# First loads and last stores of an encoder block: four DMA edits at the two ends of the kernel

## The chip, the cores and the metric

The kernel runs on one core of a Trainium2 chip. The metric is the device time of one execution in microseconds (us); where several executions are given, their median. A profile is one execution recorded by the hardware profiler; its span runs from the first to the last instruction, and its own execution time is a little longer than its span.

## The reference, cut to what matters

One encoder layer on x of 1024 tokens by 1024 channels, all float32:

```python
h = rms_norm(x, norm1_g)
a, gate, q, k, v = split(h @ w_in)             # 512 columns each
conv_out = conformer_conv(a, gate, ...)        # GLU, 31-tap depthwise conv, LayerNorm, swish
attn_out = neighbourhood_attention(rms(q), rms(k), v, rpb)
x = x + concat(conv_out, attn_out) @ w_out
h = rms_norm(x, norm2_g)
x = x + (silu(h @ w_gate) * (h @ w_up)) @ w_down    # 2816 hidden channels
```

What matters here is the first product and the last. The first product is the key projection: the transposed input (scaled by `norm1_g`) times the key columns of `w_in`. The last is `@ w_down`, whose results have the residual added and are stored to the output.

## The kernel before, in words

**Precision.** Every matmul operand is split into a high part (a rounded copy that ScalarE makes, `act.copy` or `act.activation`, L114 and L287) and a low part (the difference, made by VectorE or GpSimd, L118 and L288). A product is three matmuls: high times high (L122), high times the other's low (L123), low times high (L124), in `mac`.

**Order of the work.** The order on each engine is the order in which the code issues it (`manual_schedule`); each engine and each DMA queue works strictly in that order. "SP's queue" is the DMA queue of SyncE (`nc.sync.dma_start`), which does nothing else; "the scalar queue" is that of ScalarE (`nc.scalar.dma_start`), so a DMA there takes ScalarE's issue time. A DMA is ordered by its issue; its bytes are moved by the core's 16 DMA engines. In the profile's rows `SPq` and `ACTq` are these issues.

**The start.** `want` lists weight chunks in the order of use; `issue` loads the next chunk into one of three raw buffers (`R`, 128 x 1024, 512 KB); `take_parts` cuts the chunk's split into parts, and the last part frees the raw buffer and issues one more load. The chunks are the four key chunks `wk0` to `wk3` first, then the convolution chunks `ag10`, `ag00` and so on. `load_xt(0, kp, FIRST)` loads block kp of the transposed input: two 128-row slices of 256 tokens each (256 KB), in the tiles `xt`. `par` is a 73 KB tile of small parameters, loaded on the scalar queue; ScalarE's scaling of `xt` reads it. In the first loop over kp (0 to 3) `h_split` makes the high and low part of an `xt` slice (`hT`), the parts of the `wk` chunk are made between them, and TensorE then does the products of that kp for the first two token tiles into the accumulators `z`. The third buffer's reuse means that `wk3` can be issued only when the last part of `wk0` has been read.

After the four kp, `h_split` makes the second 256 tokens (`SECOND`), row statistics of x are taken by ScalarE and VectorE in turn (`stats1`, `head_post`), `take(1, False)` splits chunk `ag10` (high on ScalarE, low on GpSimd), and TensorE goes on with two more key tiles and then the gate product `gl`, which reads `ag10`.

**The end.** The last product of the down projection, `m4`, has four token tiles t = 0 to 3. `finish` adds each accumulator to `ou` on VectorE (L1351), and `store` writes the 128 x 512 result (256 KB) to the output. The output rows of a tile are not adjacent: `rows` takes them from a grid, so the destination of one store is a pattern of 8 by 16 rows of 512 numbers (2 KB). The four stores of `m4` are all on the scalar queue; those of the other products are on SP's.

The window loads of the attention stage, which the prediction compares with, read a source pattern of 4 by `ncol` rows of 2 KB (`ncol` 32 or 24):

```python
nc.sync.dma_start(vw[cb, g], vd.rearrange("(r c) d -> r c d", c=GW)[g * 4:g * 4 + 4, c0:c0 + ncol, :])
```

Of the kernel before, what the change touches and what calls it, by code (L numbers as in the profile page):

```python
# [13 lines left out]
P = 128  # L14
# [54 lines left out]
def body(tc, a):  # L69
    from contextlib import ExitStack  # L70
    with ExitStack() as ctx:
        build(ctx, tc, a)


def build(ctx, tc, a):
    nc = tc.nc
# [6 lines left out]
    def T(tag, shape, bufs, name, dt=F32):  # L83
        return sb.tile(shape, dt, tag=tag, bufs=bufs, name=name)

    def G(name, dt=F32):
        return T("G", [P, 1024], 22, name, dt)

    def R(name):
        return T("R", [P, 1024], 3, name)  # L90
# [4 lines left out]
    def ST(name, dt=F32):  # L95
        return T("st", [P, 512], 5, name, dt)
# [23 lines left out]
    def mac(acc, l, r, start, stop):  # L120
        (lh, ll), (rh, rl) = l, r
        pe.matmul(acc, lh, rh, start=start, stop=False, skip_group_check=True)  # L122
        pe.matmul(acc, lh, rl, start=False, stop=False, skip_group_check=True)  # L123
        pe.matmul(acc, ll, rh, start=False, stop=stop, skip_group_check=True)  # L124
# [14 lines left out]
    pos = [0, 0]  # L139
# [10 lines left out]
    def issue():  # L150
        if pos[0] < len(chunks):
            src, name, _, _, more = chunks[pos[0]]
            raws[pos[0]] = R(name + "r")
            d = raws[pos[0]]
            if len(src.shape) == 3:
                d = d.rearrange("p (k m) -> p k m", k=src.shape[1])
            nc.sync.dma_start(d, src)
            if more is not None:
                pending.append((d, more))
            pos[0] += 1  # L160

    def take(n=1, ahead=True):
        for _ in range(n):
            i = pos[1]
            while pos[0] <= i:
                issue()
            _, _, dst, sub, _ = chunks[i]
            hi, lo = dst()
            split(hi, lo, raws.pop(i), sub)
            pos[1] += 1  # L170
            if ahead and pos[0] < i + 4:
                issue()

    def take_parts(jobs, n=4, sub=pool):
        i = pos[1]
        hi, lo = chunks[i][2]()
        w = 1024 // n

        def part(o):
            sl = slice(o, o + w)  # L180
            split(hi[:, sl], lo[:, sl], raws[i][:, sl], (sub,))
            if o + w == 1024:
                raws.pop(i)
                issue()
        pos[1] += 1
        jobs.extend(lambda o=o: part(o) for o in range(0, 1024, w))
# [49 lines left out]
    x_t, xr = {}, {}  # L236
    FIRST, SECOND, ALL = slice(0, 256), slice(256, 512), slice(0, 512)

    def load_x(t):
        x_t[t] = G(f"x{t}")  # L240
        nc.sync.dma_start(x_t[t], a["x"][t * P:(t + 1) * P, :])

    def load_xt(h, kp, sl):
        if (h, kp) not in xr:
            xr[h, kp] = G(f"xt{h}{kp}").rearrange("p (k s) -> p k s", s=512)
        nc.sync.dma_start(xr[h, kp][:, :, sl], a["xt"][h, kp][:, :, sl])

    for kp in range(4):
        load_xt(0, kp, FIRST)
        if kp < 3:  # L250
            issue()
    ones = ST("ones")[:, :P]
    ident = T("ident", [P, P], 1, "ident")
    par = T("par", [P, 146], 1, "par")
    nc.scalar.dma_start(par, a["par"])
    g1 = par[:, 0:8]
    dwk = par[:, 8:132].rearrange("p (c t) -> p c t", t=CW)
    dwb, lng, lnb = par[:, 132:136], par[:, 136:140], par[:, 140:144]
# [25 lines left out]
    def h_split(h, k, sl):  # L284
        src = xr[h, k // 2][:, k % 2, sl]
        hi, lo = [w[:, k, sl] for w in hT[h]]
        act.activation(hi, src, AF.Copy, scale=g1[:, k:k + 1])  # L287
        dve.scalar_tensor_tensor(lo, src, g1[:, k:k + 1], hi.bitcast(F32), OP.mult, OP.subtract)  # L288
# [253 lines left out]
    for kp in range(4):  # L542
        parts = []
        take_parts(parts, 2, dve)
        for j in range(2):
            h_split(0, 2 * kp + j, FIRST)
            parts[j]()
        if kp == 0:
            for q in range(4):
                load_xt(0, q, SECOND)  # L550
            load_x(0)
            load_x(1)
        if kp == 2:
            load_x(2)
            load_x(3)
        for j in range(2):
            for t in range(2):
                k = 2 * kp + j
                mac(zs[t], [q[:, k, t * P:(t + 1) * P] for q in hT[0]],
                    [q[:, j * 512:(j + 1) * 512] for q in wn[1][kp]], k == 0, k == KB - 1)  # L560
# [9 lines left out]
    for q in range(4):  # L570
        load_xt(1, q, ALL)
# [280 lines left out]
    def rows(ap, t):  # L852
        rh, cb = divmod(t, 4)
        return ap.rearrange("(h i w) d -> h i w d", h=2, w=GW)[rh, :, cb * 16:cb * 16 + 16, :]
# [309 lines left out]
    gt, bank, sl, u2, late = {}, {}, {}, {}, []  # L1164
# [160 lines left out]

    def store(p, t, w):
        tok, d = {"m2": (0, 0), "m3": (0, 1), "m4": (1, 0), "m7": (1, 1)}[p]
        (nc.scalar if p == "m4" else nc.sync).dma_start(
            rows(a["out"], 4 * tok + t)[:, :, d * 512:(d + 1) * 512], w)

    def quarter(w, o, t):
        return w[:, o + t * 512:o + t * 512 + 512]
# [1 line left out]
    def finish(p, t):  # L1334
        acc = (GA if p in ("m1", "m2", "m7", "m4") else GB)[t]
        if p == "m1":
            if t == 0:
                om["m1"] = H("om1")
            (dve.tensor_copy, act.copy)[t % 2](quarter(om["m1"], 2048, t), acc)
        elif p == "m2":  # L1340
            dve.tensor_tensor(res[p, t], acc, res[p, t], OP.add)
            store(p, t, res[p, t])
        elif p == "m6":
            if t == 0:
                om["u"] = H("ou")
            dve.tensor_tensor(quarter(om["u"], 0, t), acc, quarter(om["m1"], 2048, t), OP.add)
        elif p == "m5":
            dve.tensor_tensor(quarter(om["u"], 2048, t), acc, quarter(om["m1"], 2048, t), OP.add)
        else:
            w = {"m7": quarter(om["u"], 2048, t), "m3": quarter(om["m1"], 2048, t), "m4": quarter(om["u"], 0, t)}[p]  # L1350
            dve.tensor_tensor(w, acc, w, OP.add)  # L1351
            store(p, t, w)
# [48 lines left out]
```

## Time and profile before

| | us |
|---|---|
| Time, median of 3 runs (1049.48 to 1050.58) | 1049.9 |
| The profiled execution's own time | 1050.14 |
| Its span, first to last instruction | 1048.4 |
| TensorE busy (98% of the span) | 1028.2 |
| VectorE busy (69%) | 722.9 |
| ScalarE busy (44%) | 465.3 |
| GpSimd busy (43%) | 452.6 |

The granted TensorE clock is 0.999 over the span. The times of rows in the timeline count from the span's start; a row gives start, duration, engine, line, operation, output and inputs, and in brackets the idle time before it with what ended it. The DMA share is the mean busy share of the 16 DMA engines, so 0.50 means as much work as eight engines kept busy. TensorE's busy time counts pipelined matmuls, whose ends are modelled.

### The profile page before, as it was taken

What the parts mean: (1) busy time and instruction counts of PE and PEld (TensorE: products, weight loads), DVE (VectorE), ACT (ScalarE), POOL (GpSimd) and SP (SyncE); (2) the same over time, 40 slices, a digit from 0 to 9 for tenths busy, and PEclk for the clock granted to TensorE, in tenths of its full rate; (3) what the DMA queues carried; (4) which work ended last, traced back from release to release, by engine and by line L of the source; (5) the groups of instructions that cost most, each with busy time, mean ns of one, the idle gap of its engine ahead of it and who ended that gap; (6) DMA issues with size and microseconds to landing.
All of it is one profiled execution on the core that took longest, in us unless ns stands there. A gap on an engine that the chain in (4) does not pass through costs nothing.

```text
span 1048.4 us, 13903 instructions
## 1 busy us (share of the span) xinstructions
PE 1028.2 (98%) x4972; PEld 833.8 (80%) x4972; DVE 722.9 (69%) x1097; ACT 465.3 (44%) x915; POOL 452.6 (43%) x342
## 2 busy tenths in 40 slices
PE   7999999999999999999999999999999999999997
PEld 5888888776657888778888888888888888888885
DVE  6768998976896575876564655646556567768883
ACT  6466346636776676532232232232322443443441
POOL 0226578833575863655545454455454100002310
PEclk9999999999999999999999999999999999999999
DMA  9496771285536754465232132232232597633641
GB/s 334 178 271 220 225 238 61 77 244 168 148 109 163 159 182 141 109 167 174 104 131 101 71 131 101 89 132 93 99 111 81 207 326 256 205 101 125 215 133 40
DMA packets 74678, 162.93 MB, mean 155 GB/s; under 512 B 13489, under 2 KB 22193, under 8 KB 73905
## 3 DMA queue, kind: packets, MB, share of 16 engines
q1 hardware_dynamic: 67776, 144.14, 40.7%
q0 software_dynamic: 4864, 10.49, 5.9%
q10 hardware_dynamic: 1968, 7.42, 2.0%
q8 instruction: 39, 0.64, 0.2%
q14 instruction: 31, 0.25, 0.1%
HBM read 122.86 MB, written 53.15 MB: 168 GB/s over the span
## 4 chain that ended last, share of the span: by engine, by line
PE 88%; DVE 4%; POOL 2%; DMA 2%; ACT 2%; issue 2%; SPq 0%; POOLq 0%; ACTq 0%; DVEq 0%
PE B L122 5%; PE B L123 5%; PE B L124 5%; PE D L123 4%; PE D L124 4%; PE D L122 4%; PE A L122 3%; PE A L123 3%; PE A L124 3%; PE z L123 3%; PE z L122 3%; PE z L124 3%; PE gl L124 3%; PE gl L123 3%; PE gl L122 3%; PE n L122 3%
## 5 line engine op out<-in xcount | busy, mean ns | idle before, releaser
L347 DVE SCALAR_TENSOR_TENSOR cv<-u,par,cv 128x1009 f32<-128x1009 f32 (+14 forms) x85 | 108.5, 1276 | 2.0
L373 POOL TENSOR_TENSOR pa<-pa,pr 128x1022 f32<-128x1022 f32 (+10 forms) x31 | 75.2, 2426 | 33.7 <-ACT pr L372 32.2
L1356 POOL TENSOR_TENSOR ou<-ou,resm 128x512 f32<-128x512 f32 x8 | 12.5, 1571 | 142.5 <-DMA resm<-xd 142.5
L114 ACT CAST op<-sr 128x512 fp32r<-128x512 f32 x77 | 47.7, 619 | 52.7 <-PE B2d L124 21.3
L118 DVE TENSOR_TENSOR op<-sr,op 128x512 fp32r<-128x512 f32 x77 | 58.2, 756 | 16.4 <-ACT op L114 16.4
L1193 DVE TENSOR_TENSOR g<-B,g 128x512 f32<-128x512 f32 x22 | 15.2, 690 | 71.3 <-PE B L124 68.2
L1202 ACT ACTIVATE D<-D 128x512 f32<-128x512 f32 x22 | 12.8, 582 | 112.5 <-DVE D L1201 112.5
L1185 DVE TENSOR_TENSOR u<-B,g 128x512 f32<-128x512 f32 x22 | 15.2, 691 | 61.0 <-PE B L124 61.0
L668 POOL TENSOR_SCALAR e<-e,rs 128x288 f32<-128x288 f32 (+1 forms) x64 | 35.0, 568 | 45.6 <-DVE rs L666 41.0
L114 ACT CAST op<-wd 128x512 fp32r<-128x512 f32 x66 | 40.9, 620 | 30.4 <-DVE wd L1280 17.4
L118 DVE TENSOR_TENSOR op<-wd,op 128x512 fp32r<-128x512 f32 x66 | 50.5, 765 | 1.9 <-ACT op L114 0.3
L986 DVE TENSOR_TENSOR ts<-ts,gu 128x512 f32<-128x512 f32 x36 | 43.3, 1203 | 0.6
L1191 ACT ACTIVATE A<-A 128x512 f32<-128x512 f32 x18 | 10.5, 582 | 68.6 <-PE A L124 68.6
L661 ACT ACTIVATE e<-e,mx 128x288 f32<-128x288 f32 (+1 forms) x64 | 36.3, 569 | 2.9 <-DVE mx L659 2.8
L659 DVE CUSTOM_DVE_ANT_0 e<-s,tab 128x288 f32<-128x288 f32 (+1 forms) x64 | 29.7, 501 | 8.7 <-PE s L646 8.4
L372 ACT ACTIVATE pr<-u,par 128x1022 f32<-128x1022 f32 (+10 forms) x31 | 34.2, 1135 | 1.2 <-ACT vs L433 1.2
L677 PEld LDWEIGHTS p<-ident,e 128*96 128x96 f32 (+1 forms) x192 | 20.0, 133 | 18.1 <-POOL e L668 10.4
L677 PE MATMUL p<-ident,e 128*96 128x128 f32 (+1 forms) x192 | 28.5, 281 | 2.3 <-DVE pT L682 1.0
L986 DVE TENSOR_TENSOR ts<-gu 128x512 f32<-128x512 f32 x18 | 30.1, 1670 | 0.0
L865 DVE TENSOR_TENSOR x<-x,n 128x512 f32<-128x512 f32 x32 | 21.0, 681 | 13.1 <-PE n L124 13.1
L693 PE MATMUL o<-pT,vw 96*64 96x128 f32 (+1 forms) x384 | 28.0, 281 | 0.0
L646 PE MATMUL s<-kT,qT 64*128 64x288 f32 (+1 forms) x128 | 26.7, 495 | 0.0
(1066 smaller groups left out, 3524.1 us busy)
## 6 DMA issues: line engine op xcount, KB each, us to landing
sr<-sd SPq DMA_DIRECT2D x77, 256.0 KB
gu<-in_gu SPq DMA_DIRECT2D x36, 512.0 KB
sd<-sd SPq DMA_DIRECT2D x22, 512.0 KB
wd<-in_wd SPq DMA_DIRECT2D x44, 256.0 KB
sd<-g SPq DMA_DIRECT2D x33, 256.0 KB
x<-in_x SPq DMA_DIRECT2D x12, 512.0 KB
xd<-x SPq DMA_DIRECT2D x8, 512.0 KB
resm<-xd SPq DMA_DIRECT2D x16, 256.0 KB
```

The source lines that it names most:

```text
L114: act.copy(hi, src)
L118: eng.tensor_tensor(*[w[..., sl] for w in (lo, src, hi.bitcast(F32))], OP.subtract)
L122: pe.matmul(acc, lh, rh, start=start, stop=False, skip_group_check=True)
L123: pe.matmul(acc, lh, rl, start=False, stop=False, skip_group_check=True)
L124: pe.matmul(acc, ll, rh, start=False, stop=stop, skip_group_check=True)
L347: dve.scalar_tensor_tensor(acc[:, o], uc[:, i], dwk[:, c, t:t + 1], acc[:, o], OP.mult, OP.add)
L372: act.activation(pr[:, o], uc[:, i], AF.Copy, scale=dwk[:, c, t:t + 1])
L373: pool.tensor_tensor(pa[:, o], pa[:, o], pr[:, o], OP.add)
L661: act.activation(e[:, hh], e[:, hh], AF.Exp, bias=mx, scale=-1.0, accum_out=rs[:, hh:hh + 1])
L668: pool.tensor_scalar(es[i][:, hh], es[i][:, hh], rs[:, hh:hh + 1], 1.0, op0=OP.mult, op1=OP.mult)
L677: pe.transpose(pt[:m, g * P:(g + 1) * P], es[i][:, hh, g * m:(g + 1) * m], ident)
L986: dve.tensor_tensor(lr(tsum[i, 1])[n - 3] if o is None else o, l, r, OP.add)
```

## The change

Four edits, and the code of the products is not touched.

1. The first weight chunk `wk0` is loaded in two DMAs of 128 x 512, and these now stand ahead of everything else on SP's queue.
2. The first input block `xt` (kp = 0) goes from SP's queue to the scalar queue, behind `par`, which is issued earlier in the code. For kp = 1 and 2 the weight chunk is now issued ahead of the input block instead of behind it.
3. For the first half of kp = 0 the weight part is made before the input slice's split, instead of after it.
4. Of the four `m4` stores t = 0 and 2 stay on the scalar queue, t = 1 goes to SP's, and t = 3 is cut in two stores of 64 partitions, one on each queue; each half's destination has 4 by 16 rows.

```diff
             if len(src.shape) == 3:
                 d = d.rearrange("p (k m) -> p k m", k=src.shape[1])
-            nc.sync.dma_start(d, src)
+            for o in (0, 512) if pos[0] == 0 else (None,):
+                nc.sync.dma_start(*[w if o is None else w[:, o:o + 512] for w in (d, src)])
             if more is not None:
...
-    def load_xt(h, kp, sl):
+    def load_xt(h, kp, sl, eng=nc.sync):
         if (h, kp) not in xr:
             xr[h, kp] = G(f"xt{h}{kp}").rearrange("p (k s) -> p k s", s=512)
-        nc.sync.dma_start(xr[h, kp][:, :, sl], a["xt"][h, kp][:, :, sl])
-
+        eng.dma_start(xr[h, kp][:, :, sl], a["xt"][h, kp][:, :, sl])
+
+    par = T("par", [P, 146], 1, "par")
+    nc.scalar.dma_start(par, a["par"])
     for kp in range(4):
-        load_xt(0, kp, FIRST)
         if kp < 3:
             issue()
+        load_xt(0, kp, FIRST, nc.sync if kp else nc.scalar)
     ones = ST("ones")[:, :P]
     ident = T("ident", [P, P], 1, "ident")
-    par = T("par", [P, 146], 1, "par")
-    nc.scalar.dma_start(par, a["par"])
...
         for j in range(2):
-            h_split(0, 2 * kp + j, FIRST)
-            parts[j]()
+            both = [parts[j], lambda: h_split(0, 2 * kp + j, FIRST)]
+            for f in both if kp == j == 0 else both[::-1]:
+                f()
...
     def store(p, t, w):
         tok, d = {"m2": (0, 0), "m3": (0, 1), "m4": (1, 0), "m7": (1, 1)}[p]
-        (nc.scalar if p == "m4" else nc.sync).dma_start(
-            rows(a["out"], 4 * tok + t)[:, :, d * 512:(d + 1) * 512], w)
+        out = rows(a["out"], 4 * tok + t)[:, :, d * 512:(d + 1) * 512]
+        if (p, t) == ("m4", 3):
+            nc.sync.dma_start(out[:4], w[:64])
+            nc.scalar.dma_start(out[4:], w[64:])
+        else:
+            (nc.scalar if p == "m4" and t % 2 == 0 else nc.sync).dma_start(out, w)
```

How this moves instructions: SP's queue at the start of the program, before (the sizes are those of the tile that is written; `xt_73`, `xt_77`, `xt_81` and `xt_85` are the input blocks of kp 0 to 3):

```order
L246 DMA xt_73<-in_xt 128x2x256
L157 DMA wk0r<-in_qkv 128x1024
L246 DMA xt_77<-in_xt 128x2x256
L157 DMA wk1r<-in_qkv 128x1024
L246 DMA xt_81<-in_xt 128x2x256
L157 DMA wk2r<-in_qkv 128x1024
L246 DMA xt_85<-in_xt 128x2x256
L157 DMA wk3r<-in_qkv 128x1024
```

The same place in the changed kernel (`xt_82`, `xt_86` and `xt_88` are the blocks of kp 1 to 3):

```order
L158 DMA wk0r<-in_qkv 128x512 x2
L158 DMA wk1r<-in_qkv 128x1024
L247 DMA xt_82<-in_xt 128x2x256
L158 DMA wk2r<-in_qkv 128x1024
L247 DMA xt_86<-in_xt 128x2x256
L247 DMA xt_88<-in_xt 128x2x256
L158 DMA wk3r<-in_qkv 128x1024
```

Seven loads still stand ahead of `wk3`'s, as before; block 0 has left the queue, and `wk1` and `wk2` have moved ahead of their blocks.

ScalarE at the start, as one piece of the difference (`xt_78` is block 0 in the changed kernel):

```order
-L255 DMA par<-in_par 128x146
-L263 ACT_TABLE_LOAD
-L263 ACTIVATE warm<-eps 128x1
-L287 ACTIVATE hT_69<-xt_73,par 128x256
+L250 DMA par<-in_par 128x146
+L247 DMA xt_78<-in_xt 128x2x256
+L264 ACT_TABLE_LOAD
+L264 ACTIVATE warm<-eps 128x1
 L114 CAST wk0h<-wk0r 128x512
-L287 ACTIVATE hT_69<-xt_73,par 128x256
+L288 ACTIVATE hT_69<-xt_78,par 128x256 x2
 L114 CAST wk0h<-wk0r 128x512
```

ScalarE issues the load of block 0 itself, ahead of its table load, and its first work on data is now the first half of `wk0` instead of block 0.

SP's queue and ScalarE at the end of the changed kernel, SP first. In the kernel before, ScalarE's end is a single row, `out_dram<-ou 8x16x512 x4`, and SP's queue ends with the row of `sr`:

```order
L1254 DMA sr_8500<-sd 128x512
L1254 DMA sr_8542<-sd 128x512 x2
L1254 DMA sr_8580<-sd 128x512
L1335 DMA out_dram<-ou 8x16x512
L1332 DMA out_dram<-ou 4x16x512
```

```order
L114 CAST op_8617<-wd_7447 128x512
L114 CAST op_8652<-sr_8580 128x512
L114 CAST op_8652<-wd_7471 128x512
L1335 DMA out_dram<-ou 8x16x512 x2
L1333 DMA out_dram<-ou 4x16x512
```

Two destinations of 8 by 16 rows are left on the scalar queue, one is on SP's, and each queue ends with one of 4 by 16 rows.

## The prediction

> **What bounds the kernel now.** I read the page's engine shares first, then TensorE's waits, then the timeline of the first 34 us and of the last 10 us, and the DMA rows there.
>
> ```profile
> PE 1028.2 (98%) x4972; PEld 833.8 (80%) x4972; DVE 722.9 (69%) x1097; ACT 465.3 (44%) x915; POOL 452.6 (43%) x342
> PE z L122 <- ACT wk0h L114: 7.3, 1, 7.3
> PE B L122 <- DVE u L1185: 1.4, 1, 1.4
> PE gl L124 <- POOL ag10l L118: 0.2, 1, 0.2
> ```
>
> TensorE is the bound: of the 20.2 us in which it isn't busy (1048.4 - 1028.2), 7.3 are the wait for the first operand, 7.0 lie behind its last matmul (which ends at 1041.35, below), and the other 5.9 are short waits in the middle. The change touches only the first two. But the last row matters as much: at 33 us TensorE already waits 0.2 us for something that is not its own doing. What starts TensorE earlier gains nothing that this wait takes back.
>
> The start, in the timeline (start, duration, engine, line; idle before it in brackets):
>
> ```profile
> 0.79 0.71 SPq L246 DMA_DIRECT2D xt<-in_xt  x1
> 0.80 0.40 ACTq L255 DMA_DIRECT2D par<-in_par  x1
> 1.56 0.57 SPq L157 DMA_DIRECT2D wk0r<-in_qkv  x1
> 4.38 0.51 ACT L287 ACTIVATE hT<-xt,par 128x256 fp32r<-128x256 f32 x1 [1.65 <-DMA xt<-in_xt]
> 6.67 0.62 ACT L114 CAST wk0h<-wk0r 128x512 fp32r<-128x512 f32 x1 [1.78 <-DMA wk0r<-in_qkv]
> 7.34 0.79 PE L122 MATMUL z<-wk0h,hT 128*128 128x512 f32 x1 [7.34 <-ACT wk0h L114]
> 8.32 0.68 DVE L118 TENSOR_TENSOR wk0l<-wk0r,wk0h 128x512 fp32r<-128x512 f32 x1
> 8.81 0.62 ACT L114 CAST wk1h<-wk1r 128x512 fp32r<-128x512 f32 x1 [0.19 <-DMA wk1r<-in_qkv]
> 9.04 0.34 SPq L157 DMA_DIRECT2D wk3r<-in_qkv  x1
> 10.83 0.62 ACT L114 CAST wk2h<-wk2r 128x512 fp32r<-128x512 f32 x1
> 12.28 0.51 ACT L287 ACTIVATE hT<-xt,par 128x256 fp32r<-128x256 f32 x1
> 13.84 0.62 ACT L114 CAST wk3h<-wk3r 128x512 fp32r<-128x512 f32 x1 [1.06 <-DMA wk3r<-in_qkv]
> 15.29 3.31 ACT L287 ACTIVATE hT<-xt,par 128x256 fp32r<-128x256 f32 x8
> 29.44 1.04 ACT L114 CAST ag10h<-ag10r 128x1024 fp32r<-128x1024 f32 x1
> 30.56 2.38 POOL L118 TENSOR_TENSOR ag10l<-ag10r,ag10h 128x1024 fp32r<-128x1024 f32 x1 [29.20 <-DMA xt<-in_xt]
> 33.00 0.50 PE L124 MATMUL gl<-hT,ag10l 128*128 128x512 f32 x1 [0.21 <-POOL ag10l L118]
> ```
>
> TensorE starts when `wk0` has landed and its first half is cast. From then to 33.00 it has one gap, the 0.21 us before `gl`. The other way to 33.00 runs over ScalarE and VectorE: the cast of `wk3` waits for its DMA until 13.84, then come eight more splits, the statistics in turns, the cast of `ag10` (ends 30.48), GpSimd's low part (30.56 to 32.94). The page names a DMA before that GpSimd row, but ScalarE's cast ended 0.08 us before it, and I take the cast as the cause. From 13.84 to 33.00 I treat this chain as stiff, 19.2 us.
>
> The end (PEclk, DMA share and GB/s are the last columns of the stretches):
>
> ```profile
> 1038.03 4.69 ACTq L1328 DMA_DIRECT2D out_dram<-ou  x4
> 1040.96 0.39 PE L124 MATMUL A3d<-op 128*128 128x512 f32 x1
> 1041.39 0.69 DVE L1351 TENSOR_TENSOR ou<-A3d,ou 128x512 f32<-128x512 f32 x1 [0.67 <-PE A3d L124]
> 1041.00:1046.00 5.00, 0.35 (x2) 0.00 (x0) 0.69 (x1) 0.00 (x0) 0.00 (x0) 0.96 0.50 163
> 286.00:289.00 3.00, 2.74 (x26) 1.70 (x24) 2.90 (x14) 2.08 (x7) 1.94 (x4) 1.00 0.26 102
> ```
>
> Of the stretch 1041 to 1046 us the DMA share is 0.50, the work of eight engines, at 163 GB/s: 20.4 GB/s for each. A store's destination has 8 as its outermost count. The window loads in flight from 286 to 289 us have 4 outermost, and there the share is 0.26 and the rate 102 GB/s, four engines at 25.5 GB/s. So the outermost count sets how many engines work, and the stores are held by their eight engines:
>
> ```profile
> DMA  0000026534254555445445544454545453100000
> GB/s 0 0 0 0 0 57 82 41 25 57 98 197 180 197 180 131 98 156 205 188 172 180 131 115 172 172 172 164 164 115 180 180 197 148 41 0 0 0 0 0
> ```
>
> These are the 40 slices of 0.25 us from 1038 to 1048. The first store is issued at 1038.03 and its first bytes move in the slice from 1039.25, about 1.25 us later. Bytes move until the slice that ends at 1046.75, with no pause at the end, so the last store waits behind the three ahead of it.
>
> **The change part by part: the start.** Loads before `wk3`: 73 + 256 + 512 + 256 + 512 + 256 + 512 + 256 KB before and after, only in another order, and the loads of SP that stand ahead of it are seven in both.
>
> When can TensorE start? Before, 329 KB (`par`, block 0) had landed by 4.38 and 841 KB by 6.67, about 224 KB per us. The first matmul now needs `par`, half of `wk0` and block 0, 585 KB in all; at that rate they land at 4.38 + 256/224 = 5.5. If block 0 on its own queue shares so badly that the whole of `wk0` goes first, it is 6.67. The cast of the half chunk (0.62) is over by then, ahead of block 0 in ScalarE's order; block 0's split takes 0.51. So TensorE starts between 6.0 and 7.2 instead of 7.34. I take 6.1, as the two queues are fed from the same time (0.79 and 1.2): TensorE is 1.2 us earlier.
>
> What is late next is `gl` at 33.00. If TensorE comes 1.2 us earlier and the other chain doesn't move, the wait before `gl` grows from 0.21 to 1.4 and the gain is nothing. So what counts is how much earlier the cast of `wk3` gets. From above: ScalarE takes four operations per kp, from `wk2`'s cast at 10.83 to the end of the row at 12.28, 1.96 us. Block 1 now comes behind `wk1`, where `wk1` stood, so its split can't start much before 8.8; two kp of 1.96 and one split of 0.51 later it is 13.2, against 13.84: a gain of at most 0.6. From below: `wk3`'s load is issued when the last read of `wk0` ends (8.32 + 0.68, issue at 9.04); it now ends about 0.5 to 1 earlier, but the same bytes still stand in front of it. The stretch from 7 to 20 us has the DMA engines full:
>
> ```profile
> 7.34:11.20 3.86, 3.86 (x8) 2.76 (x9) 3.80 (x8) 3.60 (x8) 0.00 (x0) 1.00 1.02 365
> 11.20:20.00 8.80, 8.80 (x40) 7.28 (x39) 7.24 (x17) 7.68 (x18) 0.00 (x0) 1.00 1.00 363
> ```
>
> With the share at 1.00 an earlier issue mostly queues. A loss could come from the two half loads, which move 2 KB runs instead of 4 KB and are one issue more; 512 KB at 365 GB/s are 1.44 us, and a fifth of that, 0.3, is my bound. Between +0.3 and -0.6 I take **-0.2 us** for the whole start. Edits 1 to 3 thus come to little, although TensorE starts over a microsecond earlier.
>
> **The end.** Stores t = 0 to 2 keep their pattern of eight outer rows. Moving t = 1 to SP's queue saves nothing by itself if the same engines carry both queues: the limit is engine time, and SP's queue has nothing behind its last `sr` load. It does not save issue time on the path either, since four issues took 4.69 us in all, spread by VectorE's adds. The two halves of t = 3 each have 4 outermost, so each gets four engines. Successive window loads on one queue never went above 0.26 while more than one was in flight (four were issued from 278.81 on, and the share is still 0.26 at 286 to 289):
>
> ```profile
> 278.81 6.30 SPq L631 DMA_DIRECT2D vw<-vd  x4
> vw<-vd SPq DMA_DIRECT2D x4, 256.0 KB
> ```
>
> So a small pattern always takes the same four engines, at least on one queue. No row shows two queues. If the two halves take the same four, these carry 3 x 32 + 64 = 160 KB each instead of 128: 32 KB more at 20.4 GB/s is +1.6 us; if four busy engines run at the window loads' 25.5 GB/s, the last 64 KB take 2.57 instead of 1.61, +0.96. The store's rate is the nearer row (same direction, same rows), so I take **+1.4**. If the halves take different engines, each engine's work stays as it was.
>
> The Trainium skill, "DMA: Bandwidth & Descriptors", section "Why a DMA increments its semaphore by 16 and not by 1", says that a DMA uses the largest number of engines up to 16 that divides the slowest dimension of both patterns, and on these two queues always the lowest-numbered ones. The trace agrees for 8 and 4 (0.50 and 0.26); that two queues take the same ones no run here shows; by it the end would be the +1.4 as taken, by its denial the first rival below. The rules for kernel authors on that page of the Trainium skill also advise against splitting one transfer into two partition halves.
>
> **The sum.** 1050.14 (the profiled execution) - 0.2 + 1.4 = 1051.3. The median of the runs is 0.24 lower than that execution, so I forecast **1051.1** for the median, 0.1% above before. A measurement of this kernel can tell about 0.2%, 2.1 us, from no change.
>
> **The rivals.**
> *The end gains.* If SP's stores and the two halves run on other engines than those of the scalar queue, nothing waits behind a store: the last halves are issued at 1042.1, first bytes 1.25 us later, then 1.61 for 32 KB per engine, 1045.0 against 1046.75: -1.8. With the start 1049.9 - 1.8 - 0.2 = 1047.9. For it: eight engines idle during the stores. Against it: the window loads left twelve idle and never used them. 0.16.
>
> *The start passes in full.* If `ag10` moves with TensorE by 1.2, the time is 1049.9 - 1.2 + 1.4 = 1050.1. For it: the chain waits for a DMA at 13.84. Against it: ScalarE's own 1.96 us per kp. 0.08.
>
> *The halves do nothing.* Four engines alone write fast enough, or the halves spread: end 0, 1049.7. 0.06.
>
> *The start loses, on the slower side.* Block 0 on the scalar queue shares the engines with SP's weights and gets less than half of them. ScalarE and VectorE work in order and hold the second half of `wk0` behind it: two splits, a cast and a low part, about 2.3 us from block 0's landing to the issue of `wk3` (before, 2.37 from 6.67 to 9.04). So it decides from a landing at 6.7 on. Before, block 0 landed 2.9 us after its issue ended at 1.50, 0.7 of it for 256 KB at 365 GB/s; with a fifth of that rate they take 3.6, and from an issue that ends at 1.8 it lands at 1.8 + 2.2 + 3.6 = 7.6. Then `wk3` is issued at 9.9, 0.9 late, and with 1.5 at the end it is 1049.9 + 2.4 = 1052.3. For it: `wk0` and `wk1` now stand ahead on SP's queue. Against it: its own queue holds only 73 KB in front. 0.09.
>
> **How the numbers follow.** The forecast has 0.61, with its own range 1050.3 to 1051.8 (start -0.6 to +0.3, end +0.96 to +1.6). The range 1047.9 to 1052.0 leaves out half of the first rival and most of the last, under 0.2. Faster by over 0.2% (under 1047.8) is the lower half of the first rival, 0.10 with what I don't know; slower by over 0.2% (over 1052.0) the last rival with the top of the forecast, 0.10; the rest 0.80.
>
> **What would show it.** In the changed profile TensorE's first matmul near 6.1; a wait of over 1 us at `gl` for the low part of `ag10`, which ends at 32.5 to 33.2; from 1045.5 a DMA share near 0.25 with bytes until about 1048. A last byte near 1045 proves the first rival; a `gl` wait of under 0.3 with `ag10` done by 32 the second; `wk3`'s issue after 9.3 the last. I am wrong if the share stays at 0.5 or goes above it while the halves move.

## The result, and the profile after

| | before | after |
|---|---|---|
| Time, median of 4 runs (lowest to highest), us | 1049.69 (1049.26 to 1050.58) | 1069.48 (1068.70 to 1070.18) |
| Profiled execution, us | 1050.14 | 1068.7 |
| Its span, us | 1048.4 | 1067.0 |

The ratio is 1.0184, with a 95% interval of 1.0171 to 1.0196: the change costs 19.8 us where 1.2 were forecast (1051.1 against 1049.9), and the time lies far above the range of 1047.9 to 1052.0.

The row to read first is that of the engines' shares, now of the changed kernel:

```profile
PE 1045.9 (98%) x4972; PEld 835.6 (78%) x4972; DVE 720.3 (68%) x1097; ACT 465.6 (44%) x915; POOL 453.9 (43%) x342
```

TensorE executes the same 4972 matmuls as before and is busy 17.7 us longer (1045.9 - 1028.2). The span is 18.6 us longer (1067.0 - 1048.4), so nearly all of the loss isn't idle time, and no wait can explain it. The granted clock over the span is 0.999 as before. The waits of the changed kernel, TensorE's longest first, confirm it:

```profile
PE z L122 <- ACT hT L288: 7.5, 1, 7.5
PE B L122 <- DVE u L1187: 1.1, 1, 1.1
```

The wait for the first operand is 7.5 instead of 7.3, and the one for `u` is 1.1 instead of 1.4.

Where do the 17.7 us arise? The view of a tile gives, for each group of instructions, the shortest, median and longest duration in ns and the first and last start in us. These are rows of three products before: the first of the gate and up stage (`A<-h,t0m`; the stage makes `h @ w_gate` and `h @ w_up`), a later one of that stage (`D<-S,t0m`) and one of the down projection (`B1d<-op`).

```profile
L122 PE MATMUL A<-h,t0m x8: 389/432/477, 406.4 to 416.6; 128*128 128x512 f32 x8
L122 PE MATMUL D<-S,t0m x4: 389/389/389, 443.8 to 445.9; 128*128 128x512 f32 x4
L122 PE MATMUL B1d<-op x33: 389/389/395, 891.9 to 1007.9; 128*128 128x512 f32 x33
```

The same three rows after:

```profile
L122 PE MATMUL A<-h,t0m x8: 394/438/481, 412.1 to 422.5; 128*128 128x512 f32 x8
L122 PE MATMUL D<-S,t0m x4: 392/396/400, 449.8 to 451.9; 128*128 128x512 f32 x4
L122 PE MATMUL B1d<-op x33: 389/389/395, 909.1 to 1025.1; 128*128 128x512 f32 x33
```

The loss is 5.7 us where the gate and up stage begins (412.1 - 406.4), 17.2 where the down projection begins (909.1 - 891.9), and still 17.2 at its last `B1d` (1025.1 - 1007.9). The matmuls of the middle take a few ns longer each; those of the down projection take what they took. So it is a slower pace, in some products and not in others.

A stretch in which TensorE never stops shows the pace best. The columns are the stretch and its length, then busy time and, in brackets, the number of instructions of TensorE, its weight loads, VectorE, ScalarE and GpSimd, then the granted clock, the DMA share and GB/s. The first stretch lies in the gate and up stage, the second in the down projection. Before:

```profile
500.00:800.00 300.00, 300.00 (x1325) 248.43 (x1324) 171.40 (x207) 86.35 (x157) 150.37 (x111) 1.00 0.29 103
860.00:1000.00 140.00, 139.98 (x618) 115.55 (x617) 106.80 (x152) 59.24 (x106) 19.39 (x12) 1.00 0.54 180
```

After:

```profile
500.00:800.00 300.00, 300.00 (x1288) 242.19 (x1287) 162.01 (x199) 84.76 (x155) 146.58 (x108) 1.00 0.29 103
860.00:1000.00 140.00, 139.97 (x618) 115.55 (x617) 103.09 (x152) 59.50 (x106) 12.89 (x8) 1.00 0.57 194
```

In 300 us TensorE starts 1325 matmuls before (226.4 ns each) and 1288 after (232.9 ns each), at a granted clock of 1.00 in both; in the down projection it starts 618 in both (226.5 ns). Below, "count" is the number of matmuls in the stretch from 500 to 800.

The rest of the loss is at the end. After the end of VectorE's last addition (1041.39 + 0.69 = 1042.08 before, in the prediction) the span went on for 6.3 us; now it goes on for 1067.0 - 1059.29 = 7.7:

```profile
1058.60 0.69 DVE L1357 TENSOR_TENSOR ou<-A3d,ou 128x512 f32<-128x512 f32 x1 [0.67 <-PE A3d L124]
1059.32 0.56 SPq L1332 DMA_DIRECT2D out_dram<-ou  x1
1059.32 0.56 ACTq L1333 DMA_DIRECT2D out_dram<-ou  x1
```

### The profile page after: what moved, and what is told of

It reads as the page before. It is cut to its first block, busy times and chain, and to the rows that moved or that the text cites. A ratio compares the mean times of both kernels' runs of the same rounds, so it can differ in the third digit from the quotient of the medians.

```text
span 1067.0 us, 13908 instructions
## 1 busy us (share of the span) xinstructions
PE 1045.9 (98%) x4972; PEld 835.6 (78%) x4972; DVE 720.3 (68%) x1097; ACT 465.6 (44%) x915; POOL 453.9 (43%) x342
## 4 chain that ended last, share of the span: by engine, by line
PE 90%; DVE 3%; POOL 2%; issue 2%; ACT 2%; DMA 1%; ACTq 0%; POOLq 0%; DVEq 0%
PE B L124 5%; PE B L122 5%; PE B L123 5%; PE z L122 4%; PE z L123 4%; PE z L124 4%; PE D L123 4%; PE D L124 4%; PE D L122 4%; PE A L122 3%; PE A L123 3%; PE A L124 3%; PE gl L123 3%; PE gl L122 3%; PE gl L124 3%; PE n L122 2%
## 5 line engine op out<-in xcount | busy, mean ns | idle before, releaser
L118 DVE TENSOR_TENSOR op<-sr,op 128x512 fp32r<-128x512 f32 x77 | 58.3, 757 | 16.0 <-ACT op L114 15.8
L373 ACT ACTIVATE pr<-u,par 128x1022 f32<-128x1022 f32 (+10 forms) x31 | 34.2, 1135 | 1.2 <-ACT vs L434 1.2
```

The source lines that it names most:

```text
L118: eng.tensor_tensor(*[w[..., sl] for w in (lo, src, hi.bitcast(F32))], OP.subtract)
L373: act.activation(pr[:, o], uc[:, i], AF.Copy, scale=dwk[:, c, t:t + 1])
```

## What the edit of `par` also does

The second edit moves the line `par = T("par", [P, 146], 1, "par")` ahead of the first loads. That line issues nothing: it is the allocation of a tile. But a group of buffers gets its place in SBUF, the on-chip memory of all tiles, in the order in which the groups are first asked for. In the programs as they were built (the profile shows no addresses) the order before is the `H` group (six buffers of 16 KB per partition, from byte 16512), then `G` (22 buffers of 4 KB, from byte 114816); after, `par` stands between the two (584 bytes, which take 608), and `G` begins at 115424. Every distance between an `H` buffer and a `G` buffer was a multiple of 256 bytes (114816 - 16512 = 384 x 256) and is now 96 more than one (608 = 2 x 256 + 96).

The transposed input `hT` and `h2` of the products lie in `H`; the weights (`wk`, `ag`, and the `t` of the gate and up stage) lie in `G`. In the down projection both operands, all `op`, lie in `H`. So the products that got slower are those with one operand in each group.

The gate and up stage holds a test of this inside the one trace. It makes seven products for each block of hidden channels. One operand of each is a `t` in `G`; the other lies in `H`, but for the sixth product, whose `S4` lies in `G` too (`s_split`). These rows of the changed kernel are the first matmuls of the fourth to the seventh product of block 13, twelve matmuls apart:

```profile
680.74 0.39 PE L122 MATMUL B<-S,t13m 128*128 128x512 f32 x1
683.55 0.40 PE L122 MATMUL D<-S,t13m 128*128 128x512 f32 x1
686.36 0.39 PE L122 MATMUL B<-S,t13m 128*128 128x512 f32 x1
689.09 0.40 PE L122 MATMUL D<-A,t13m 128*128 128x512 f32 x1
```

The fourth and the fifth take 2.81 us, 234 ns a matmul. The sixth, with both operands in `G`, takes 2.73, 227 ns, although `G` lies where the slow ones have it. In the kernel before, the products of this block take 2.72.

Four readings of this were to be told apart. Theory A: `G` begins at an address that is off by 32 bytes from a multiple of 64. Theory B: the new order of the DMAs, or of the tiles in memory, does it. Theory C, formed when A fell: what counts is the distance of a matmul's two operands, modulo some power of two, and not the address of either. And the change's own edits at the start and the end could have a part that only looks like a slow pace. The letters in the expectations are those of the time at which each was written.

## Experiments on the pace

**The change, with `par` padded to 640 bytes**, so that `G` begins on a multiple of 64 again.

```diff
-    par = T("par", [P, 146], 1, "par")
+    par = T("par", [P, 160], 1, "par")[:, :146]
```

> The changed kernel with one thing more: par's tile is 160 columns wide (640 bytes per partition) of which 146 are used, so that the tiles allocated behind it start at a multiple of 64 bytes again (115456) instead of 32 beyond one (115424). All DMAs and the order stay those of the change. Theory A (TensorE reads operands whose address is 32 beyond a multiple of 64 bytes more slowly): the matmul pitch goes back to 227 ns, the 17 us disappear, 1050 to 1052 us (what is left is the end's +1.4 and the start). Theory B (the new DMA order or the new order of the tiles in memory does it): stays at 1069.

1066.94 us against 1050.7, ratio 1.0156 (1.0139 to 1.0173). Its stretch from 500 to 800:

```profile
500.00:800.00 300.00, 300.00 (x1292) 242.23 (x1291) 164.02 (x202) 84.16 (x153) 146.91 (x108) 1.00 0.30 103
```

The count is 1292 instead of 1288: hardly better, where 1050 to 1052 us was expected by theory A. It fell with this run.

**The kernel before, with only the allocation moved** ahead of the first loop. The load of `par` and every other instruction stay where they were.

```diff
+    par = T("par", [P, 146], 1, "par")
     for kp in range(4):
         load_xt(0, kp, FIRST)
...
-    par = T("par", [P, 146], 1, "par")
     nc.scalar.dma_start(par, a["par"])
```

> The kernel before with only the line that allocates par's tile moved ahead of the first loads; its DMA and everything else stay where they were. Theory A: all tiles behind par are at 32 beyond a multiple of 64, TensorE's busy time rises by some 17 us: 1065 to 1068 us. Theory B (DMA order): 1049.9, as no DMA has moved.

1066.97 against 1050.7, 1.0155 (1.0140 to 1.0171), +16.3 us. This is the run that decides on the cause's place: without one instruction changed or moved, the kernel loses 16.3 us, and the whole change lost 19.8. No DMA has moved, so the part of theory B that is about DMAs falls. The page's engine shares:

```profile
PE 1046.0 (98%) x4972; PEld 835.1 (78%) x4972; DVE 720.7 (68%) x1097; ACT 465.5 (44%) x915; POOL 453.5 (43%) x342
```

Its stretch from 500 to 800:

```profile
500.00:800.00 300.00, 300.00 (x1288) 242.21 (x1287) 161.93 (x199) 84.29 (x154) 146.87 (x108) 1.00 0.30 103
```

TensorE's busy time and the count are those of the changed kernel.

**The same with 640 bytes.**

```diff
+    par = T("par", [P, 160], 1, "par")[:, :146]
     for kp in range(4):
...
-    par = T("par", [P, 146], 1, "par")
```

> As the run that only moves par's tile to the front, but with the tile 640 bytes wide: the same order in memory, addresses at multiples of 64. Theory A: 1049.9, no different from before. If the place of par ahead of the others matters by itself: 1065 or more.

1064.49, 1.0133 (1.0118 to 1.0148), +13.8, where theory A had no loss. TensorE is busy for 1043.7 us and the count is 1292: 2.3 us less busy time than with 608 bytes, so the size of the loss depends on the distance, but 128 modulo 256 is still slow.

**The kernel before with an unused tile of 32 bytes** between the groups.

```diff
+    T("pad", [P, 8], 1, "pad")
     for kp in range(4):
```

> The kernel before with an unused tile of 32 bytes per partition ahead of the first loads; par stays behind. Theory A: the same 32-byte shift by another means, 1065 to 1068 us. If it is not the shift but par's own place: 1049.9.

1065.36, 1.0139 (1.0124 to 1.0155), +14.7. A tile that nothing reads or writes costs nearly as much:

```profile
500.00:800.00 300.00, 300.00 (x1291) 242.12 (x1290) 162.56 (x200) 84.05 (x153) 147.32 (x109) 1.00 0.30 103
```

So neither `par`'s contents nor the engines that read it are needed for the loss. But a tile ahead of `G` shifts all that is allocated behind it as well: the raw buffers `R`, `ident`, `par` and others. Two runs part the groups.

**32 bytes ahead of `H` too**: everything from `H` on is shifted by the same 32 bytes.

```diff
+    T("pad", [P, 8], 1, "pad")
     hT = [[H(f"hT{h}{w}", F32R).rearrange("p (k s) -> p k s", s=512) for w in range(2)] for h in range(2)]
```

> The kernel before with the unused 32-byte tile ahead of all tiles, the large H tiles too. Theory A, refined: each matmul that reads one operand at 32 beyond a multiple of 64 is some 6 ns slower; now both operands of all products are, and the down projection's too, which stayed at 227 ns in the changed kernel. If the losses of the two operands add: 1080 to 1095 us. If one such operand is as bad as two: about 1071 to 1075, as only the stages that were spared are added.

1050.54 against 1050.47, 1.0001 (0.9992 to 1.0010): no loss, where the expectation had one of 20 us or more.

```profile
500.00:800.00 300.00, 300.00 (x1326) 248.48 (x1324) 171.05 (x206) 86.35 (x157) 150.44 (x112) 1.00 0.30 104
```

`G` begins 32 bytes off where it began before, exactly as in the run above, and the pace is the full one, because `H` has moved with it. A rule on the address of `G` alone can't give both results, and one on that of `H` alone can't part the kernel before from the one with 32 bytes between (`H` is at the same place in both).

**32 bytes behind `G`**, ahead of the raw buffers, `ident` and `par`.

```diff
+    xr[0, 0] = G("xt00").rearrange("p (k s) -> p k s", s=512)
+    T("pad", [P, 8], 1, "pad")
     for kp in range(4):
```

> The kernel before with the unused 32-byte tile between the G tiles and the rest: the raw buffers R, the 2 KB tiles, the identity and par are shifted, the G and H tiles (all matmul operands of the products) are not. Theory A (only what TensorE reads matters): 1049.9 to 1051, since of TensorE's operands only the transposes' are shifted. If ScalarE's, VectorE's or the DMAs' access to shifted tiles matters: clearly slower, up to 1067.

1050.67, 1.0001 (0.9992 to 1.0011), count 1325. Shifting the groups behind `G` costs nothing. What is left is the distance between `H` and `G`.

**512 bytes between the groups**: the identity tile, 128 x 128 numbers, is allocated ahead of `G`.

```diff
+    ident = T("ident", [P, P], 1, "ident")
     for kp in range(4):
...
-    ident = T("ident", [P, P], 1, "ident")
```

> The kernel before with only the 512-byte identity tile allocated ahead of the G tiles instead of behind them; no DMA and no instruction moves. Theory C (the pitch depends on the distance between the addresses of a matmul's two operands, taken modulo 512 bytes: distances of 0 are fast, 32, 96 and 128 are slow, and a shift of all operands together is harmless): 512 is 0 again, so 1050.5 as before. If any tile between the H and the G tiles slows TensorE, whatever its size: 1064 to 1067.

1050.42 against 1050.2, 1.0003 (0.9994 to 1.0012).

**256 bytes between the groups**: small tiles that the kernel has anyway, and 32 bytes of filling.

```diff
+    eps = T("eps", [P, 1], 1, "eps")
+    qgs = T("qgs", [P, 1], 1, "qgs")
+    r1 = T("r1", [P, 8], 1, "r1")
+    T("bn", [P, 2, 6], 2, "bn0")
+    T("pad", [P, 8], 1, "pad")
     for kp in range(4):
```

> The kernel before with small tiles of 256 bytes together ahead of the G tiles, so that G lies 256 bytes further from H. If the period of the distance is 256: 1050.5 as before, the pitch 227 ns. If it is 512: slow like 32, 96 and 128, 1063 to 1067, pitch of the mixed products 232 to 234 ns.

1050.4, 1.0003 (0.9994 to 1.0012).

```profile
500.00:800.00 300.00, 300.00 (x1325) 248.40 (x1324) 171.10 (x207) 86.40 (x157) 150.18 (x111) 1.00 0.30 103
```

The count is 1325 in both. All distances tried, with the time lost in runs of otherwise the same kernel:

| shift of `G` against `H`, bytes | modulo 256 | count in 500 to 800 | ns per matmul | time against before, us |
|---|---|---|---|---|
| 0 | 0 | 1325 | 226.4 | |
| 256 | 0 | 1325 | 226.4 | +0.2 |
| 512 | 0 | 1325 | 226.4 | +0.2 |
| 32 | 32 | 1291 | 232.4 | +14.7 |
| 608 | 96 | 1288 | 232.9 | +16.3 |
| 640 | 128 | 1292 | 232.2 | +13.8 |

A count is good to about one matmul, 0.2 ns. All six fit a period of 256 bytes in the distance (256 and 512 are as fast as 0), and a period of 128 or less that is a power of two is out (640 is 128 more than 512, and slow). A longer period with several fast distances in it is not excluded. What in the chip makes it so, no run shows; that stays open. Distances such as 64, 160 or 192 were not tried.

## Experiments on the start and the end

**The change with `par`'s tile behind `G`.** The four edits are all there; only the allocation's place is put back, by asking for block 0's `G` buffer first.

```diff
+    xr[0, 0] = G("xt00").rearrange("p (k s) -> p k s", s=512)
     par = T("par", [P, 146], 1, "par")
     nc.scalar.dma_start(par, a["par"])
```

> The changed kernel, all four edits, with par's tile allocated behind the G tiles instead of ahead of them; its DMA stays at the front. Theory C: the 17 us are gone; the stores keep their +1.4 to +2.1 (their run alone), the start adds 0 to +1 (first matmul at 7.2 to 8.5 in the runs with the new start, 6.1 to 7.3 with the old): 1051.5 to 1053.5. If the change has another cost that only shows in its full form: over 1055.

1054.2 against 1050.2, ratio 1.0036 (1.0024 to 1.0049), +4.0 us: the 17 us are gone, but the time is above the 1051.5 to 1053.5 that was expected. The page's engine shares:

```profile
PE 1028.7 (98%) x4972; PEld 834.5 (79%) x4972; DVE 726.1 (69%) x1097; ACT 465.4 (44%) x915; POOL 452.1 (43%) x342
```

Its stretch from 500 to 800:

```profile
500.00:800.00 300.00, 300.00 (x1325) 248.51 (x1324) 170.46 (x205) 86.98 (x159) 150.18 (x111) 1.00 0.31 105
```

TensorE's busy time is back at 1028.7 and the count at 1325: the place of `par` is 15.8 of the 19.8 us, within half a us of the 16.3 of the allocation alone. What was predicted of the edits is to be held against the +4.0; the padded change less the allocation with the same 640 bytes, from runs made side by side, gives 1066.94 - 1064.49 = 2.45 for the same edits, at the slow pace. Its start, in the timeline:

```profile
4.07 0.62 ACT L114 CAST wk0h<-wk0r 128x512 fp32r<-128x512 f32 x1 [0.63 <-DMA wk0r<-in_qkv]
8.00 0.91 ACT L289 ACTIVATE hT<-xt,par 128x256 fp32r<-128x256 f32 x2 [3.31 <-DMA xt<-in_xt]
8.56 0.80 PE L122 MATMUL z<-wk0h,hT 128*128 128x512 f32 x1 [8.56 <-ACT hT L289]
10.16 0.33 SPq L158 DMA_DIRECT2D wk3r<-in_qkv  x1
13.71 0.62 ACT L114 CAST wk3h<-wk3r 128x512 fp32r<-128x512 f32 x1 [0.20 <-DMA wk3r<-in_qkv]
```

The half chunk has landed by 4.07, but block 0, alone behind `par` on the scalar queue, lands only at 8.00, and ScalarE waits 3.31 us for it.

**The end alone**: the kernel before with the change's `store`.

```diff
+        if (p, t) == ("m4", 3):
+            nc.sync.dma_start(out[:4], w[:64])
+            nc.scalar.dma_start(out[4:], w[64:])
+        else:
+            (nc.scalar if p == "m4" and t % 2 == 0 else nc.sync).dma_start(out, w)
```

> The kernel before with only the stores of the change (t = 1 on SP's queue, t = 3 in halves of 4 by 16 rows on two queues). If both halves run on the same four engines: the time behind VectorE's last add grows by 1.0 to 1.6 us, 1050.9 to 1051.4. If the queues' engines differ: 1047.9 to 1048.3.

1052.62 against 1050.47, 1.0022 (1.0013 to 1.0031), +2.15 us: a loss as by the first branch of the expectation, but larger. The stretches of the end, whose last three columns are clock, DMA share and GB/s:

```profile
1041.00:1043.00 2.00, 0.00 (x0) 0.00 (x0) 0.55 (x1) 0.00 (x0) 0.00 (x0) 1.00 0.54 185
1044.00:1047.00 3.00, 0.00 (x0) 0.00 (x0) 0.00 (x0) 0.00 (x0) 0.00 (x0) 0.62 0.25 70
```

While whole stores move, the share is 0.54; when the two halves are left, it is 0.25, on two queues. Its DVE row `ou<-A3d` ends at 1041.55 and the span at 1049.6, 8.05 behind it, against 6.3 before. In the four profiles with these stores it is 7.6 to 8.5, in the nine with the stores of before 6.1 to 6.35, so against the profile before the new end cost 1.3 to 2.1 us.

**The start alone**: the change with 640 bytes of `par` and the stores of the kernel before.

```diff
-        out = rows(a["out"], 4 * tok + t)[:, :, d * 512:(d + 1) * 512]
-        if (p, t) == ("m4", 3):
...
+        (nc.scalar if p == "m4" else nc.sync).dma_start(
+            rows(a["out"], 4 * tok + t)[:, :, d * 512:(d + 1) * 512], w)
```

> The changed kernel's start alone (the first three edits), with par's tile 640 bytes wide and the stores of before. The changed profile shows TensorE starting at 7.52 instead of 7.34, but the cast of wk3 at 12.62 instead of 13.84. If the late first matmul decides: +0.2, 1050.1. If the wait before gl decides (0.21 us before): nothing from it can be gained that TensorE does not have, so between 1049.7 and 1050.1; that is no difference that can be told.

1065.73, 1.0146 (1.0132 to 1.0159), +15.3. The expectation took the padded tile to be harmless, which it is not: the run has the slow pace of the 640-byte shift (count 1292), so it is to be compared with the run that has that shift alone, +13.8: about 1.5 us for the start. By the other pair, the change with `par` behind `G` (+4.0) less the end alone (+2.15), it is 1.85. The padded pair (2.45) less the end alone leaves only 0.3. The intervals of such differences are 1.6 to 2.6 us either way, so the times alone make a loss likely and leave its size open. The traces point the same way: TensorE begins at 7.2 to 8.6 in the four profiles with the new start and at 6.1 to 7.3 in the nine with the old one.

**A version meant to beat both**: `wk0` in two loads but behind block 0 on SP's queue, the stores t = 0 to 2 as before, the last store in eight of 16 partitions each, in turn on the two queues.

```diff
+            for o in (0, 512) if pos[0] == 0 else (None,):
+                nc.sync.dma_start(*[w if o is None else w[:, o:o + 512] for w in (d, src)])
...
+        if (p, t) == ("m4", 3):
+            for i in range(8):
+                (nc.sync, nc.scalar)[i % 2].dma_start(out[i], w[16 * i:16 * i + 16])
```

> The kernel before with wk0 loaded in halves (both behind block 0 on SP's queue, as wk0 was) and the last store cut into eight stores of 16 rows, four on each queue; a destination of 16 rows outermost should put each of them on all 16 engines. If so, the engines that are idle behind the other stores take half of the last one, and its landing comes 0.8 to 1.6 us earlier; the start gains 0 to 0.5: 1048.6 to 1049.9. If eight issues cost more than they save: 1050.5 to 1052.

1050.48 against 1050.2, 1.0006 (0.9997 to 1.0015): no gain, where up to 1.6 us were hoped for. TensorE starts at 5.85, the earliest of all runs, and its last addition still ends at 1041.81, 0.27 earlier than before. The end in the timeline:

```profile
1041.12 0.69 DVE L1356 TENSOR_TENSOR ou<-A3d,ou 128x512 f32<-128x512 f32 x1 [0.67 <-PE A3d L124]
1041.84 3.67 SPq L1332 DMA_DIRECT2D out_dram<-ou  x4
1041.85 2.58 ACTq L1332 DMA_DIRECT2D out_dram<-ou  x4
```

And the stretch in which the DMA engines are busiest:

```profile
1044.00:1045.00 1.00, 0.00 (x0) 0.00 (x0) 0.00 (x0) 0.00 (x0) 0.00 (x0) 1.00 0.84 258
```

The small stores do use more engines (share 0.84, 258 GB/s, against 0.50 and 163 for the stores before), but the eight issues take until 1045.5 (1041.84 + 3.67), and the span ends 6.3 us behind the addition, as before. None of the versions tried is faster than the kernel before.

## Why the prediction was wrong, and where it was right

**The step that failed** stands in the sum: "1050.14 (the profiled execution) - 0.2 + 1.4". It takes the 1028.2 us of TensorE's work as given and changes only what lies before its first matmul and behind its last; "the change touches only the first two" of its idle times was as far as the change was followed. The part by part list treats `par` as a load that is issued earlier, and not as an allocation that comes earlier too. That term was costed at nothing without being named, and it measured +16.3 us alone. None of the rivals contained it, and a range made of stalls couldn't hold it: each of the rivals is a few us of waiting at an end of the kernel, while a few ns on each of thousands of matmuls have no row in the list of waits. The size fits: by the code some 2600 of the 4972 matmuls have one operand in each group (576 in the three projections, 384 in `gl`, 1584 in gate and up, 48 of the first output product), and 17.7 us over 2600 is 6.8 ns each, against the 7 (234 - 227) of block 13. What could have been seen beforehand is that one allocation moves the address of every buffer allocated behind it; what it costs could not be read from the profile of before.

**The end: the mechanism held, the size nearly.** The forecast was +1.4, from bounds of +0.96 and +1.6, on the reading that a small pattern takes the same four engines whichever queue it is on. The time from the last addition to the end of the span grew by 1.4 us in the changed kernel's profile (7.7 - 6.3), and by 1.7 in that of the end alone; the median of the end alone grew by 2.15 (interval about 1.4 to 3.3), so the forecast lies at the low side of what was measured. The DMA rows of the changed kernel, 40 slices from 1056 to 1067 us, and the two queues' shares in them (q10 has 0.66 MB, two and a half of the four stores, so it is the scalar queue's):

```profile
DMA  0047252554654545644542312222222100000000
q10 hardware_dynamic: 340, 0.66, 19.9%
q1 hardware_dynamic: 204, 0.39, 10.7%
```

And the stretch of the last bytes, clock, DMA share and GB/s at its end:

```profile
1061.50:1064.50 3.00, 0.00 (x0) 0.00 (x0) 0.00 (x0) 0.00 (x0) 0.00 (x0) 0.89 0.27 87
```

With both halves in flight the share is 0.27, the work of four engines of 16 between the two queues. This is the row that the prediction lacked for two queues. It speaks for what the Trainium skill says in "DMA: Bandwidth & Descriptors", section "Why a DMA increments its semaphore by 16 and not by 1", that these queues use the lowest-numbered engines: with 0.27 on two queues, and not 0.50, the trace agrees that both use the same four, though not which four they are. The rivals "the end gains" and "the halves do nothing" fall with it.

**The start: the likeliest case was wrong, and the last rival came in part.** The forecast had block 0 at 5.5 and TensorE at 6.1, "as the two queues are fed from the same time". In the changed kernel block 0 landed before 6.96 and TensorE began at 7.52:

```profile
1.24 0.67 ACTq L247 DMA_DIRECT2D xt<-in_xt  x1
3.90 0.62 ACT L114 CAST wk0h<-wk0r 128x512 fp32r<-128x512 f32 x1 [0.46 <-DMA wk0r<-in_qkv]
6.96 0.91 ACT L288 ACTIVATE hT<-xt,par 128x256 fp32r<-128x256 f32 x2 [2.44 <-DMA xt<-in_xt]
7.52 0.80 PE L122 MATMUL z<-wk0h,hT 128*128 128x512 f32 x1 [7.52 <-ACT hT L288]
9.13 0.33 SPq L158 DMA_DIRECT2D wk3r<-in_qkv  x1
```

With `par` behind `G` it landed at 8.00 and TensorE began at 8.56. What the two queues (q1 is SP's, q10 the scalar queue) moved in that run from 2 to 7.6 us:

```profile
q1 hardware_dynamic: 736, 1.51, 75.3%
q10 hardware_dynamic: 416, 0.34, 20.0%
```

The scalar queue moved 0.34 MB (`par` and block 0) beside SP's 1.51, 18% of the bytes. So the block got a small part of the rate beside SP's loads, as the rival "the start loses" had it with its fifth and its landing at 7.6. A landing from 6.7 on was to decide (6.96 and 8.00), and `wk3` is issued after 9.3 in the run with `par` behind `G` (10.16; the changed kernel has 9.13, short of it). The rival's time of 1052.3 against 1049.9, +2.4 for start and end together, compares with +4.0 for the change with `par` behind `G` (2.5 to 5.1), or 2.45 by the padded pair. One link of it did not hold: `wk3` is issued 1.1 us later than before and is cast at 13.71 against 13.84, no later at all. What costs there is plainer: TensorE itself starts 1.2 us later than in the profile of before, it does not wait at `gl`, and it reaches the first `gl` that reads `ag10`'s low part at 34.2 instead of 33.0.

The gain was also counted from an execution that began late. Among the runs whose first matmul still waits for `wk0` whole, it comes between 6.1 and 7.3 us, and the 7.34 of the profile before is the latest of nine; without any edit of the start the end-alone run began at 6.34.

**The wait at `gl`** could not show itself as predicted, since TensorE did not start early. Where it did, the reading bears up: these are rows of the waits of the run with 32 bytes behind `G`.

```profile
PE z L122 <- ACT wk0h L114: 6.2, 1, 6.2
PE gl L124 <- POOL ag10l L118: 1.3, 1, 1.3
```

It starts 1.1 us earlier than the profile before and waits 1.1 longer at `gl`: an earlier TensorE alone gained nothing, as the prediction had it. The end-alone run, which starts at 6.34, and the version with 16-partition stores, at 5.85, wait less than 0.1 us there, and this also fits: in them ScalarE cast `wk3` at 12.77 and 12.90 instead of 13.84, and GpSimd's low part of `ag10` ended 19.1 us behind that cast, as in the profile before (32.94 - 13.84). So the chain is as stiff as the prediction took it in all ten profiles with block 0 first on SP's queue; what moves from one execution to the next is the cast of `wk3` from which it starts.

**The sum, as it should have stood**: +16.3 for the place of `par`, about +2 for the end, and for the start something between 0.3 and 1.85, the least sure term; together 18.6 to 20.2, measured +19.8.

## What to carry to other kernels

A moved allocation is an edit of its own: before costing a change, list which buffers change their address with it, and compare TensorE's count of matmuls in a saturated stretch before looking at any wait. Here matmuls were fast where their operands lay a multiple of 256 bytes apart and slow at the three other distances tried, so a small tile goes behind the large groups or is padded to a multiple of 256 bytes. A store cut in two by partitions, on two queues, gets no more DMA engines when each half has a smaller outermost count (the share fell to 0.25 to 0.27), and a load that the first work needs should not compete from another queue with loads that aren't yet needed.

## What the runs showed that was not expected

The pace of a matmul depends on where its operands lie to each other: 226.4 ns with one group shifted by 0, 256 or 512 bytes against the other, 232.2 to 232.9 with 32, 608 or 640, and 300/1326 = 226.2 with both shifted by 32. The granted clock is 1.00 in all of these stretches, so it is not the clock. And a 256 KB load on the scalar queue, issued at 1.24 beside five loads that SP's queue began to issue by 2.9, had landed by 6.96 in one run and only at 8.00 in another, though the half chunk of the same size that SP issued first had landed by 3.90 and 4.07.
